# The last additions to x in each mixer: every second one through ScalarE and GpSimd

## The chip, the cores and the metric

The kernel runs on one core of a Trainium2 chip. A core has TensorE (PE, with its weight loads PEld), VectorE (DVE), ScalarE (ACT), GpSimd (POOL) and SyncE (SP), which issues most DMAs. Each engine takes its instructions in the order in which they were written out; semaphores hold one engine back for another. The metric is the device time of one execution in microseconds. Three runs of the kernel before gave 2718.03, 2725.59 and 2727.16 us; the median is 2725.59 us.

## The reference

Two layers work on x, 256 tokens of 2048 features. Layer 0 mixes tokens by sparse attention, layer 1 by an RWKV-7 recurrence, and each mixer is followed by an MLP. What matters here is how a mixer ends and the MLP begins:

```python
    y = mixer(hmix)                       # ends in  o @ w_o
    x = x + g1 * y
    hff = rms_norm(x) * (1 + sc2) + sh2
    x = x + g2 * (jnp.square(jax.nn.relu(hff @ mlp_w1[i])) @ mlp_w2[i])
```

All is float32. The factors g1, sc2 and sh2 come from the conditioning vector through a large matrix (adaLN).

## The kernel before

x lies in SBUF as 16 tiles (x0 to x15, 128 features x 256 tokens). Every float32 product is made of three matmuls: an operand is split into a rounded upper half (hi) and the rest (lo), and the product is hi·hi + hi·lo + lo·hi (`acc3`, L184 to L186). A weight tile is loaded in pieces of 128x512; ScalarE casts each to its hi half (L92), and VectorE or GpSimd subtracts to get its lo half (L94).

The end of a mixer is `out_group` (L451): a block of columns of o times w_o gives 128x256 in PSUM, and L457 on VectorE multiplies it by g1 and adds it to x[f]. The sum over o is cut into blocks, so each x[f] is added to several times, 160 additions in all. The last pass over f = 0 to 15 is the one after which the MLP may use x: in layer 0 the pass over one last tile of o (L732 to L735), in layer 1 the pass over the last two (L841 to L846). In layer 0 the products use five PSUM buffers (`kinds` is `TAIL`), in layer 1 two (`kinds` is "d").

The MLP (`mlp`, L362) needs of each x[f]: h, that is x times a factor in its two halves (hi by L376 on ScalarE, lo by L377 on VectorE), two more columns of h that hold the shift (L372 and L373, GpSimd); and the sum of squares over all f (`tally`: square by L311 on ScalarE, addition by L313 on GpSimd). Each of its first products (`up`, 48 matmuls over the 16 tiles of h) can start before the sum of squares is known, because the norm is applied after it; the root (L289) and its spreading to all partitions (L304 on TensorE) come later. Beside this the adaLN factors of later layers are worked out on VectorE: the sigmoid of c (L208, with a table load, on ScalarE), c times it (L209, 128x2048), then one reduction of 128x2048 after another (L256).

The order on each engine is not the order of the text. A scheduler writes it out from a model of the whole program's course, with priorities where `high_priority` is written. So an edit at one place can move instructions on every engine. Tiles are taken from rings of a fixed number of buffers; a ring's next user waits for its last reader.

Of the kernel before, what the change touches and what calls it, by code (L numbers as in the profile page):

```python
# [11 lines left out]
AF = mybir.ActivationFunctionType  # L12
OP = mybir.AluOpType
# [7 lines left out]
NF = D // P  # L21
# [80 lines left out]
class Trunk:  # L102
# [345 lines left out]
                down(b, g)  # L448
        turn(3)

    def out_group(s, name, layer, block, g, movs, first=0):  # L451

        w = s.wload(s.io[name][block * 4 + g, :, first * 512:(first + len(movs)) * 512])
        for o in range(4):
            f = g * 4 + o
            p = s.dense(w, movs, [k * 512 + o * P for k in range(len(movs))])
            s.nc.vector.scalar_tensor_tensor(s.x[f], p, s.m(layer, 2, f), s.x[f], op0=OP.mult, op1=OP.add)  # L457


    def angles(s, freq, which):  # L460
# [39 lines left out]
    def dsa(s):  # L500
# [65 lines left out]
        p = s.dense(w, h, [k * P for k in range(16)])  # L566
# [153 lines left out]
        last = None  # L720
        for b in range(4):
            om = []
# [7 lines left out]
            last = om  # L730
        s.kinds = TAIL
        for n, o in ((0, om[:3]), (3, om[3:])):  # L732
            for g in range(4):
                s.out_group("a_w_o", 0, 3, g, o, n)
                s.ada(ADA_OUT)  # L735


# [83 lines left out]
    def rwkv_scan(s):  # L821
        todo, om, pre = [], [], []
        for f in range(AHEAD):
            pre.append(s.prepare(f))
            if not f:
                s.pairs()
            if f < AHEAD_INV:
                s.inverse(f, pre[f])
        for f in range(NF):
            cur = pre.pop(0)  # L830
            with s.tc.high_priority(URGENT):
                s.chain(f, cur)
            if f + AHEAD_INV < NF:
                with s.tc.high_priority(URGENT):
                    s.inverse(f + AHEAD_INV, pre[AHEAD_INV - 1])
            if f + AHEAD < NF:
                pre.append(s.prepare(f + AHEAD))
            om.append(s.finish(f, cur))
            if todo and f >= LATE:
                todo.pop(0)()  # L840
            if f in CUTS:  # L841
                todo += [lambda b=f // 4, o=om, g=g, n=f % 4 + 1 - len(om): s.out_group("b_w_o", 1, b, g, o, n)
                         for g in range(4)]
                om = []
        for t in todo:
            t()  # L846
# [453 lines left out]
```

## Time and profile before

| What | Value |
|---|---|
| median of 3 runs | 2725.59 us |
| profiled execution, its own time | 2725.82 us |
| its span, first to last instruction | 2724.0 us |
| mean granted clock | 0.971 |
| PE / PEld busy | 2589.9 us (95%) / 2278.4 us (84%) |
| DVE / ACT / POOL busy | 1832.2 (67%) / 1355.9 (50%) / 1343.7 us (49%) |

The profiled execution is one more execution beside the three runs, 0.2 us above their median. A busy share is an average over the whole span: VectorE's 67% hides stretches where it has no free time. TensorE's matmuls overlap, so the start-to-start distance of two matmuls, not the length of one, says how fast it runs. The time at which a stage ends is read from the timeline, and why an engine stood still from the view of waits.

### The profile page before, as it was taken

How to read it: one execution, taken by the hardware profiler on the slowest of the kernel's cores; microseconds unless marked ns; L12 is line 12 of the kernel's file. 1: busy time of each engine (PE TensorE's matmuls, PEld its weight loads, DVE VectorE, ACT ScalarE, POOL GpSimd, SP SyncE). 2: the span in 40 equal slices, each digit the busy share in tenths (PEclk: the TensorE clock that was granted, in tenths of full speed). 3: DMA queues.
4: the chain of work that ended last, by engine and by line, in shares of the span. 5: the costliest groups of instructions: out<-in, count | busy, mean ns of one | idle time of the engine just before them, and what ended most of it. 6: DMA issues, size and time to landing. Idle time of an engine off the chain costs nothing. (4 is left out here: it accounts for less than half of the span.)

```text
span 2724.0 us, 58482 instructions
## 1 busy us (share of the span) xinstructions
PE 2589.9 (95%) x21996; PEld 2278.4 (84%) x21996; DVE 1832.2 (67%) x2964; ACT 1355.9 (50%) x2963; POOL 1343.7 (49%) x1121
## 2 busy tenths in 40 slices
PE   6899998999999999989899899999799999999997
PEld 4566688988989989879889788888689898898986
DVE  2254468999999999769877565666797354343443
ACT  3434345555555545556655343444455565564553
POOL 1333237576576675755566222233655544444454
PEclk8999999999999999989999898999899999999999
DMA  9998535989999999736476422332585655555553
GB/s 370 410 358 339 202 123 202 325 311 371 319 338 356 318 357 330 261 111 191 140 248 216 161 84 83 99 115 95 193 313 182 215 184 189 189 184 192 186 185 103
DMA packets 263452, 623.30 MB, mean 229 GB/s; under 512 B 29312, under 2 KB 43008, under 8 KB 238336
## 3 DMA queue, kind: packets, MB, share of 16 engines
q1 hardware_dynamic: 256256, 606.98, 64.2%
q10 hardware_dynamic: 6912, 12.59, 1.3%
q8 instruction: 172, 2.82, 0.4%
q14 instruction: 112, 0.92, 0.1%
HBM read 602.67 MB, written 16.78 MB: 227 GB/s over the span
## 5 line engine op out<-in xcount | busy, mean ns | idle before, releaser
L94 POOL TENSOR_TENSOR wlo<-raw,whi 128x512 fp32r<-128x512 f32 x364 | 563.7, 1557 | 538.3 <-ACT whi L92 433.4
L92 ACT CAST whi<-raw 128x512 fp32r<-128x512 f32 x856 | 517.6, 618 | 396.7 <-PE ps_d L185 117.1
L94 DVE TENSOR_TENSOR wlo<-raw,whi 128x512 fp32r<-128x512 f32 x492 | 460.1, 947 | 217.3 <-ACT whi L92 213.6
L94 POOL TENSOR_TENSOR wlo<-more,whi 128x512 fp32r<-128x512 f32 x181 | 274.7, 1520 | 292.3 <-ACT whi L92 236.7
L92 ACT CAST whi<-more 128x512 fp32r<-128x512 f32 x366 | 223.0, 618 | 187.5 <-PE ps_m L418 44.1
L256 DVE CUSTOM_DVE_ANT_0 araw<-araw,cb 128x2048 f32<-128x2048 f32 x112 | 298.1, 2662 | 2.8 <-DMA araw<-ada_w_in 2.6
L94 DVE TENSOR_TENSOR wlo<-more,whi 128x512 fp32r<-128x512 f32 (+1 forms) x185 | 183.6, 995 | 120.4 <-ACT whi L92 117.8
L184 PE MATMUL ps_d<-A,whi 128*128 128x256 f32 x656 | 194.1, 299 | 9.5 <-ACT B L911 5.4
L185 PE MATMUL ps_d<-A,whi 128*128 128x256 f32 x656 | 189.2, 289 | 4.9 <-DVE A L198 4.8
L186 PE MATMUL ps_d<-A,wlo 128*128 128x256 f32 x656 | 188.2, 287 | 0.6 <-DVE wlo L94 0.5
L401 DVE TENSOR_TENSOR A<-B,A 128x256 fp32r<-128x256 f32 x96 | 104.1, 1085 | 99.4 <-ACT A L400 99.1
L185 PE MATMUL ps_d<-h,whi 128*128 128x258 f32 x560 | 160.3, 286 | 8.5 <-DVE h L377 8.5
L184 PE MATMUL ps_d<-h,whi 128*128 128x258 f32 x560 | 159.7, 285 | 0.0
L186 PE MATMUL ps_d<-h,wlo 128*128 128x258 f32 x560 | 158.3, 283 | 0.0
L184 PE MATMUL ps_m<-h,whi 128*128 128x258 f32 x532 | 151.2, 284 | 0.0
L185 PE MATMUL ps_m<-h,whi 128*128 128x258 f32 x532 | 150.8, 284 | 0.0
L184 PEld LDWEIGHTS ps_d<-A,whi 128*128 128x128 f32 x656 | 126.6, 194 | 28.9 <-issue 7.0
L397 ACT ACTIVATE B<-B,sm 128x256 f32<-128x256 f32 x128 | 65.1, 508 | 172.1 <-DVE B L396 172.0
L186 PE MATMUL ps_m<-h,wlo 128*128 128x258 f32 x532 | 149.9, 282 | 0.0
L185 PEld LDWEIGHTS ps_d<-A,whi 128*128 128x128 f32 x656 | 127.1, 194 | 9.1 <-DVE A L198 7.4
L186 PEld LDWEIGHTS ps_d<-A,wlo 128*128 128x128 f32 x656 | 127.1, 194 | 1.9 <-DVE wlo L94 1.0
L94 POOL TENSOR_TENSOR xlo<-more,xhi 128x512 fp32r<-128x512 f32 x51 | 102.0, 2000 | 45.5 <-ACT xhi L92 43.8
(541 smaller groups left out, 8176.4 us busy)
## 6 DMA issues: line engine op xcount, KB each, us to landing
araw<-ada_w_in SPq DMA_DIRECT2D x192, 1024.0 KB, 7.2
raw<-mlp_w_in SPq DMA_DIRECT2D x614, 256.0 KB, 4.2
more<-mlp_w_in SPq DMA_DIRECT2D x410, 256.0 KB, 4.3
raw<-b_w_r_in SPq DMA_DIRECT2D x64, 256.0 KB, 3.2
raw<-b_w_k_in SPq DMA_DIRECT2D x64, 256.0 KB, 3.5
raw<-b_w_v_in SPq DMA_DIRECT2D x64, 256.0 KB, 3.6
raw<-b_w_o_in SPq DMA_DIRECT2D x64, 256.0 KB, 3.3
hd<-A ACTq DMA_DIRECT2D x48, 256.0 KB, 4.0
```

The lines of the kernel that those rows point to most:

```text
L92: t.nc.scalar.copy(hi[:, :n], r)
L94: e.tensor_tensor(lo[:, :n], r, hi[:, :n].bitcast(F32), op=OP.subtract)
L184: mm(out, wh, m[:, :w], start=i == 0, stop=False)
L185: mm(out, wh, m[:, w:], start=False, stop=False)
L186: mm(out, wl, m[:, :w], start=False, stop=i == n - 1)
L256: nc.vector.tensor_tensor_reduce(out=w, in0=w, in1=s.cb, scale=1.0, scalar=0.0, op0=OP.mult, op1=OP.add, accum_out=acc[:, k:k + 1])
L397: nc.scalar.activation(r, u, AF.Relu, bias=c)
L401: nc.vector.tensor_tensor(t[:, S:], q, t[:, :S].bitcast(F32), op=OP.subtract)
```

## The change

In the last pass of each mixer the additions for odd f are made by two instructions: ScalarE scales the product from PSUM into a new tile of the ring B, and GpSimd adds that tile to x[f]. The even ones stay on VectorE. These are 16 of the 160 additions, 8 in each layer.

```diff
-    def out_group(s, name, layer, block, g, movs, first=0):
+    def out_group(s, name, layer, block, g, movs, first=0, last=False):
...
-            s.nc.vector.scalar_tensor_tensor(s.x[f], p, s.m(layer, 2, f), s.x[f], op0=OP.mult, op1=OP.add)
+            if last and f % 2:
+                q = s.B()
+                s.nc.scalar.activation(q, p, AF.Copy, scale=s.m(layer, 2, f))
+                s.nc.gpsimd.tensor_tensor(s.x[f], s.x[f], q, op=OP.add)
+            else:
+                s.nc.vector.scalar_tensor_tensor(s.x[f], p, s.m(layer, 2, f), s.x[f], op0=OP.mult, op1=OP.add)
...
-                s.out_group("a_w_o", 0, 3, g, o, n)
+                s.out_group("a_w_o", 0, 3, g, o, n, last=n == 3)
```

In layer 1 the same argument is passed for the block that ends at f = 15. The scheduler writes a new order. Line numbers of the changed kernel are 5 or 6 higher from here on: the addition on VectorE is L462, the two new instructions are L459 and L460. In the names below, x_66 to x_81 are x0 to x15; araw, cb and acc belong to the adaLN reductions; wlo and xlo are lo halves of weights.

VectorE where layer 1's mixer passes to its MLP, before:

```order
L457 SCALAR_TENSOR_TENSOR x_69<-ps_d,mod_85,x_69 128x256
L209 TENSOR_TENSOR cb<-cb,araw 128x2048
L457 SCALAR_TENSOR_TENSOR x_70<-ps_d,mod_85,x_70 128x256
L377 SCALAR_TENSOR_TENSOR h<-x_68,mod_85,h 128x256
L94 TENSOR_TENSOR wlo<-more,whi 128x512
L457 SCALAR_TENSOR_TENSOR x_71<-ps_d,mod_85,x_71 128x256
L377 SCALAR_TENSOR_TENSOR h<-x_69,mod_85,h 128x256
L377 SCALAR_TENSOR_TENSOR h<-x_70,mod_85,h 128x256
L457 SCALAR_TENSOR_TENSOR x_72<-ps_d,mod_85,x_72 128x256
L256 ISA araw,acc<-araw,cb 128x2048
```

and in the changed kernel, from the last two additions on:

```order
L462 SCALAR_TENSOR_TENSOR x_78<-ps_d,mod_85,x_78 128x256
L462 SCALAR_TENSOR_TENSOR x_80<-ps_d,mod_85,x_80 128x256
L377 SCALAR_TENSOR_TENSOR h<-x_66,mod_85,h 128x256
...
L377 SCALAR_TENSOR_TENSOR h<-x_81,mod_85,h 128x256
L209 TENSOR_TENSOR cb<-cb,araw 128x2048
L256 ISA araw,acc<-araw,cb 128x2048
L256 ISA acc 128x1
L94 TENSOR_TENSOR wlo<-more,whi 128x512
L94 TENSOR_TENSOR xlo<-raw,xhi 128x512
```

The 8 additions now stand in one block, then all 16 lo halves of h, then L209 and the first reduction, and only then the lo halves of the MLP's weights; before, all of these stood mixed between the additions. Layer 0 has the same shape.

ScalarE at the same place, before:

```order
L376 ACTIVATE h<-x_67,mod_85 128x256
L311 ACTIVATE B<-x_67 128x256
L208 ACT_TABLE_LOAD
L208 ACTIVATE araw<-cb 128x2048
L376 ACTIVATE h<-x_68,mod_85 128x256
L311 ACTIVATE B<-x_68 128x256
L92 CAST whi<-more 128x512
L92 CAST whi<-raw 128x512
L376 ACTIVATE h<-x_69,mod_85 128x256
```

and in the changed kernel, where the stretch begins and where it ends:

```order
L459 ACTIVATE B<-ps_d,mod_85 128x256
L311 ACTIVATE ssq<-x_66 128x256
L459 ACTIVATE B<-ps_d,mod_85 128x256 x7
L376 ACTIVATE h<-x_66,mod_85 128x256
...
L208 ACT_TABLE_LOAD
L208 ACTIVATE araw<-cb 128x2048
L311 ACTIVATE B<-x_74 128x256
...
L311 ACTIVATE lsq<-x_81 128x256
L92 CAST whi<-more 128x512
L92 CAST xhi<-raw 128x512 x2
```

All 16 L376 and 7 L311 stand between the scalings and the table load, 8 more L311 between L208 and the first cast of a weight (L92); before, the casts stood among them.

GpSimd where layer 0's mixer passes to its MLP, before:

```order
L94 TENSOR_TENSOR wlo<-raw,whi 128x512 x4
L372 CAST h<-mod_84 128x2 x4
L373 TENSOR_TENSOR h<-mod_84,h 128x2
L372 CAST h<-mod_84 128x2
L373 TENSOR_TENSOR h<-mod_84,h 128x2
```

and in the changed kernel:

```order
L460 TENSOR_TENSOR x_71<-x_71,B 128x256
L94 TENSOR_TENSOR wlo<-raw,whi 128x512
L460 TENSOR_TENSOR x_73<-x_73,B 128x256
L460 TENSOR_TENSOR x_75<-x_75,B 128x256
L460 TENSOR_TENSOR x_77<-x_77,B 128x256
L460 TENSOR_TENSOR x_79<-x_79,B 128x256
L460 TENSOR_TENSOR x_81<-x_81,B 128x256
L372 CAST h<-mod_84 128x2 x4
L373 TENSOR_TENSOR h<-mod_84,h 128x2
```

The eight L460 of a mixer stand ahead of all of L372 and L373, and these ahead of all but one of the 14 L313. Before, nothing of the products stood on GpSimd: L372 followed lo halves of weights in layer 0 and the last work of the recurrence in layer 1. On TensorE the spreading of the root (L304) stands behind 151 matmuls of `up` in layer 0 before and behind 119 now, in layer 1 behind 119 before and 81 now. In the recurrence of layer 1 the order is also another from its start on, with the same instructions.

## Rows read from the trace of the kernel before

**Rows 1.** Busy time by stage: PE, PEld, DVE, ACT, POOL, granted clock, DMA share, GB/s.

```profile
448.75:483.10 34.35, 24.37 (x167) 23.05 (x166) 34.35 (x37) 18.24 (x44) 29.63 (x22) 0.90 0.61 212
480.00:870.00 390.00, 387.45 (x2523) 354.62 (x2522) 375.11 (x338) 208.39 (x433) 258.99 (x137) 1.00 0.94 337
1945.00:1998.65 53.65, 37.77 (x223) 34.69 (x224) 50.82 (x63) 27.65 (x57) 41.02 (x52) 0.77 0.76 267
```

**Rows 2.** Waits of PE, 441 to 484 us: total us, times, longest.

```profile
PE ps_d L185 <- DVE h L377: 7.0, 2, 3.7
PE ps_d L184 <- DVE x L457: 0.8, 2, 0.5
```

**Rows 3.** Groups by line, PE, 1945 to 1998.65: busy us, mean ns, idle before.

```profile
L184 PE MATMUL ps_d<-o,whi 128*128 128x256 f32 x30 | 11.8, 401 | 13.1 <-DVE x L457 10.1 <-ACT o L197 2.8
```

**Rows 4.** Timeline of PE, layer 0: last product, first matmul behind L304.

```profile
448.62 0.28 PE L186 MATMUL ps_m<-o,wlo 128*128 128x256 f32 x1
...
482.85 0.36 PE L184 MATMUL ps_m<-h,whi 128*128 128x258 f32 x1
```

**Rows 5.** Timeline of PE, layer 1: products, then first matmul behind L304.

```profile
1945.09 0.79 PE L184 MATMUL ps_d<-o,whi 128*128 128x256 f32 x2 [2.82 <-ACT o L197]
...
1949.26 0.37 PE L185 MATMUL ps_d<-o,whi 128*128 128x256 f32 x1
1949.47 0.28 PE L186 MATMUL ps_d<-o,wlo 128*128 128x256 f32 x1
1949.59 0.28 PE L184 MATMUL ps_d<-o,whi 128*128 128x256 f32 x1
...
1981.76 0.41 PE L186 MATMUL ps_d<-o,wlo 128*128 128x256 f32 x1
...
1998.41 0.37 PE L184 MATMUL ps_m<-h,whi 128*128 128x258 f32 x1
```

**Rows 6.** ACT: lines (ns min/median/max), and two pieces of its timeline (us).

```profile
L892 ACT ACTIVATE B<-ps_m,wa x32: 456/465/477, 1356.1 to 1492.3; 128x256 f32<-128x256 f32 x32
453.66 1.69 ACT L376 ACTIVATE h<-x,mod 128x256 fp32r<-128x256 f32 x4
455.26 1.32 ACT L311 ACTIVATE B<-x 128x256 f32<-128x256 f32 x4
L208 ACT ACT_TABLE_LOAD  x2: 1283/1283/1283, 444.2 to 1948.5; - x2
L208 ACT ACTIVATE araw<-cb x2: 1914/1916/1917, 445.5 to 1949.8; 128x2048 f32<-128x2048 f32 x2
```

**Rows 7.** DVE: lines (ns min/median/max), L256 and L94 of layer 1's handover.

```profile
L457 DVE SCALAR_TENSOR_TENSOR x<-ps_d,mod,x x138: 434/481/489, 298.0 to 1983.2; 128x256 f32<-128x256 f32 x138
L377 DVE SCALAR_TENSOR_TENSOR h<-x,mod,h x32: 467/946/1515, 443.8 to 1989.1; 128x256 fp32r<-128x256 f32 x32
L209 DVE TENSOR_TENSOR cb<-cb,araw x2: 2275/2422/2570, 448.9 to 1951.7; 128x2048 f32<-128x2048 f32 x2
L256 DVE CUSTOM_DVE_ANT_0 araw<-araw,cb x9: 2275/2279/3354, 1958.9 to 1998.6; 128x2048 f32<-128x2048 f32 x9
L94 DVE TENSOR_TENSOR xlo<-raw,xhi 128x512 fp32r<-128x512 f32 x3 | 2.0, 683 | 0.1
```

**Rows 8.** POOL: timeline, line, whole-run group, then groups of layer 0's and layer 1's handover.

```profile
1949.92 1.54 POOL L373 TENSOR_TENSOR h<-mod,h 128x2 fp32r<-128x2 f32 x10
L1132 POOL TENSOR_TENSOR fin<-fin,B x16: 724/730/1181, 1594.0 to 1943.9; 128x256 f32<-128x256 f32 x16
L94 POOL TENSOR_TENSOR wlo<-raw,whi 128x512 fp32r<-128x512 f32 x364 | 563.7, 1557 | 538.3 <-ACT whi L92 433.4
L313 POOL TENSOR_TENSOR ssq<-ssq,B 128x256 f32<-128x256 f32 x14 | 13.6, 974 | 3.3 <-DVE x L457 2.5
L313 POOL TENSOR_TENSOR ssq<-ssq,B 128x256 f32<-128x256 f32 x14 | 19.9, 1424 | 8.4 <-ACT B L311 8.0
L94 POOL TENSOR_TENSOR wlo<-raw,whi 128x512 fp32r<-128x512 f32 x4 | 8.0, 1996 | 0.0
```

More of the change, by code (lines that the diff above doesn't have):

```diff
@@ L841, in rwkv_scan @@
             if f in CUTS:
-                todo += [lambda b=f // 4, o=om, g=g, n=f % 4 + 1 - len(om): s.out_group("b_w_o", 1, b, g, o, n)
+                todo += [lambda b=f // 4, o=om, g=g, n=f % 4 + 1 - len(om), l=f == NF - 1:
+                         s.out_group("b_w_o", 1, b, g, o, n, l)
                          for g in range(4)]
```

## Prediction

> **What bounds the kernel now.** I read the busy times by stage first. In the MLP of layer 0 TensorE is busy 387 of 390 us [rows 1]; in such a stretch nothing that another engine saves counts. The two places of the change are exceptions: from the end of layer 0's products to the spreading of the root TensorE is busy 24.4 of 34.35 us, and from the start of layer 1's last products to the same point 37.8 of 53.65 us, with VectorE at 34.35 and 50.8 us, full or nearly so [rows 1]. Then I read the waits there. In layer 0 TensorE waits mainly for L377, the lo half of h (7.0 us), and 0.8 us for the additions themselves [rows 2]. In layer 1 it waits 10.1 us for the additions [rows 3], because only two PSUM buffers hold products and VectorE has reductions of 2.3 to 3.4 us [rows 7] between two additions; the products, begun at 1945.09, end at about 1982 [rows 5]. So the change touches real waits, up to 11 us of them for the additions. Whether TensorE gets the time back is decided by what comes next in the new order, so I follow each engine's queue up to one mark: the first matmul behind L304, at 482.85 us in layer 0 with 151 matmuls of `up` done, and at 1998.41 in layer 1 with 119 done [rows 4, 5].
>
> **What is removed and added.** VectorE loses 16 additions of 0.48 us [rows 7], 7.7 us in all. ScalarE gains 16 scalings; the trace has none of this form, the nearest are activations from PSUM of the same size at 0.46 us, which I take; a step of L311 at 0.33 is the bound below, VectorE's own 0.48 the one above [rows 6, 7], and between them lie 0.15 us per product, less than a PSUM buffer's slack of 0.2 worked out below. GpSimd gains 16 additions of 128x256: 0.73 us undisturbed, 1.42 where VectorE works on SBUF beside it [rows 8]. By themselves these lie beside TensorE; what counts is the queues behind them.
>
> **Layer 1.** Products: 90 matmuls (30 on each of three lines [rows 3]). 18 had started by 1949.47, 0.21 us apart at half clock, when the distance fell to 0.12 [rows 5]. With ScalarE and VectorE emptying one buffer each, 0.48 us of emptying fits beside the next product of six matmuls (0.72), so the other 72 follow at 0.12: 8.6 us, end at 1958.2 instead of 1982. That is 24 us earlier. Call this point T. From T on, ScalarE: one scaling 0.46, 16 L376 at 0.42 and 7 L311 at 0.33 (each a quarter of its row), table load 1.28, L208 1.92: T+12.7; 8 more L311: T+15.3, and only now the first cast of a weight of the MLP [rows 6]. VectorE has finished h by then; L209 waits for L208 and ends at T+15.1, the first reduction at T+17.6 (2.28, or 2.5 with its disturbed ones), the first lo half of a weight at T+18.3 [rows 7]. TensorE has nothing but two matmuls until T+15 and stands until T+18.3: of the 24 us, 18 are gone. Then 77 matmuls come before L304; some 20 of them at half clock, as the 18 were after the pause ahead of 1945.09: 20 x 0.21 + 57 x 0.12 = 11 us, T+29.4 at the earliest. GpSimd may be later: last addition T+1.2, 28 small L372 and L373 at 0.154 to T+5.5, then 14 L313 and 6 lo halves of weights mixed, and the root, which I count as one more addition. Undisturbed, the twelfth L313 ends 0.73 after its square at T+14.3, and 6 x 1.56 + 3 x 0.73 more give T+27; at the durations of this handover before, 5.5 + 12 x 1.42 + 6 x 2.0 + 3 x 1.42 = T+39 [rows 8]. Those durations were measured beside nine reductions and L209 in 53.65 us; in the new order four such stand in this stretch of about 34, 0.12 per us instead of 0.19. I take the middle, T+34: the mark falls at 1958.2 + 34 + 0.5 = 1992.7, but with 81 matmuls done instead of 119. The missing 38 cost 38 x 0.12 = 4.6: 1997.3 against 1998.4, a gain of 1.1 us. The bounds T+29.4 and T+39 give -5.7 and +3.9. SP's queue moves too: three loads for reductions now stand together ahead of the weights' next ones, and the third gets its buffer when the first reduction ends, T+17.6; the pieces behind it belong to the second and third `up` behind the mark, wanted from about T+36 on, so I cost this at nothing; without that cover it would be rival 2's sign.
>
> **Layer 0.** Here five PSUM buffers hold products, and little is won ahead: the 0.8 us of rows 2, so T = 448.74 - 0.8 = 447.9. ScalarE and VectorE have the same queue, T+15.3 and T+18.3. One difference helps: three pieces of the second `up` are ready, so TensorE has 36 matmuls before it stands; they cannot start before GpSimd, which has eight additions and a lo half in its way (8 x 0.73 + 1.56 = 7.4 us from about T-5 on, to about T+3), has written the first shift columns, and they fit into the time before T+15. Behind T+18.3 stand 79 matmuls before L304: 20 x 0.21 + 59 x 0.12 = 11.3, T+29.6. GpSimd: T+3, small ones to T+7.3, 12 L313 at this handover's 0.97 to T+18.9, 5 lo halves at 1.56 to 2.0 and 3 x 0.97 more: T+29.6 to T+32; at layer 1's 1.42, T+38.6 [rows 8]. I take T+32.5: the mark at 447.9 + 32.5 + 0.4 = 480.8 with 119 matmuls instead of 151 at 482.85; the missing 32 cost 3.8: 484.6, a loss of 1.8 us. Bounds: -1.1 and +7.9.
>
> **One rule weighed.** L377 takes 0.47 or about 0.95 us, up to 1.5, while L457, which has only one input in SBUF, never takes more than 0.49; GpSimd's additions spread from 0.73 to 1.42 on the mean [rows 7, 8]. The Trainium skill, page "SBUF — State Buffer", section "Who interferes with whom", says that a VectorE instruction with two SBUF inputs contends with a GpSimd instruction that reads SBUF, one blocking the other wholly, and one with a single SBUF input does not. By that rule the change moves eight additions per layer from a form that disturbs nobody into one that blocks L377; the durations agree with it. It is rival 2 below.
>
> **The sum.** -1.1 + 1.8 = +0.7 us on the profiled execution's 2725.8 (span 2724.0 and 1.8 around it; 0.2 above the median): 2726.5, say 2727. What VectorE saves in busy time is hidden by TensorE's full stretches. The reordered recurrence has the same matmuls; I count 0, with 3 us either way as an estimate, a quarter of the products' wait of rows 3. Added bounds: -6.8 - 3 and +11.8 + 3.
>
> **Rivals.** (1) GpSimd runs undisturbed and ScalarE's queue is hidden by more weights cast early: both handovers at their lower bound, -6.8, and one more pause (T+15 to T+18.3 in layer 1) gone: -10, 2716. For it: 24 us of earlier products in layer 1 are a large reserve. Against it: the casts stand behind 15.3 us of ScalarE's queue by the written order. (2) The shared work of GpSimd and VectorE decides: every L313 and lo half at 1.42 and 2.0 in both layers, L304 at T+39, +11.8: 2737.5. It ends slower; its place is GpSimd's queue between the last L460 and L289, and it decides from about T+34 on, when TensorE has done the matmuls ahead of L304. For it: L313 took 1.42 in layer 1; against it: fewer reductions stand there now. (3) The reordered recurrence or the full VectorE of layer 0's MLP (375 of 390 us [rows 1]) shifts more than the handovers do: 5 us either way, 2722 to 2732, still no change that can be told.
>
> **How the numbers follow.** About 0.3% (8 us) is what a measurement of this kernel can tell from no change. My forecast, near zero, 0.48; rival 3 with no visible change 0.14; rival 1 0.19; rival 2 0.19. Within 0.3% falls 0.62; faster 0.19; slower 0.19. The range reaches to the times of the two side rivals, 2716 to 2738, so that about half of what each holds lies outside.
>
> **What would show it.** Right: in layer 1 the last product near 1958, no wait of TensorE for L462, but one of 15 us or more for a cast or a lo half of a weight (L92, L94); L208 12 to 13 us behind the last scaling; L304 between T+29 and T+39 in both layers, the wait ahead of it on GpSimd's L313 or L289. Wrong: TensorE at work with `up` by T+8 in layer 1 (gain of 10 us and more), products that still wait for buffers, or times past the handovers that shift by more than 5 us.

## The result and the profile after

The changed kernel takes 2742.54 us (median of 6 runs, 2740.64 to 2749.68), the kernel before in the same comparison 2726.98 (6 runs, 2718.03 to 2730.59): a ratio of 1.0064, 95% interval 1.0045 to 1.0083. It is slower by some 16 us, where 2727 and no change were forecast, and above the range (2738). The profiled execution of after took 2749.68 us with a span of 2747.9; it is the longest of the six, so differences to before are read by stretch and not from its whole span.

What the change was to do, it did. First the busy time of after in the two short stretches of [rows 1] (same columns, and from the same events), then the groups of the scalings and of GpSimd's additions (ns minimum, median, maximum, first and last start).

```profile
448.10:491.90 43.80, 23.87 (x132) 22.79 (x132) 26.75 (x33) 22.30 (x50) 40.17 (x59) 0.73 0.60 210
1960.70:2016.90 56.20, 33.84 (x182) 31.99 (x183) 33.23 (x42) 27.23 (x59) 45.25 (x63) 0.66 0.44 150
```

```profile
L459 ACT ACTIVATE B<-ps_d,mod x11: 462/475/477, 443.3 to 1974.4; 128x256 f32<-128x256 f32 x11
L460 POOL TENSOR_TENSOR x<-x,B x16: 717/737/1184, 445.2 to 1974.9; 128x256 f32<-128x256 f32 x16
```

VectorE, full before in the first stretch (34.35 of 34.35 us), is now busy 26.75 of 43.80; the busiest helper engine is GpSimd, 40.17 of 43.80 and 45.25 of 56.20. In both stretches the mean granted clock is lower than in [rows 1], 0.73 and 0.66 instead of 0.90 and 0.77.

The next rows are PE's timeline: in layer 0 the last product, L304 and the first matmul behind it ([rows 4] before), in layer 1 the first and the last product, L304 and the first matmul behind it ([rows 5]); and the group of the layer-1 products on L184 (busy us, mean ns, idle before; [rows 3]).

```profile
447.81 0.28 PE L186 MATMUL ps_m<-o,wlo 128*128 128x256 f32 x1
...
491.53 0.60 PE L304 MATMUL ps_m<-cst,sm 128*128 128x128 f32 x4
491.89 0.37 PE L184 MATMUL ps_m<-h,whi 128*128 128x258 f32 x1
...
1960.70 0.58 PE L184 MATMUL ps_d<-o,whi 128*128 128x256 f32 x1 [2.82 <-ACT o L197]
...
1974.06 0.28 PE L186 MATMUL ps_d<-o,wlo 128*128 128x256 f32 x1
...
2016.57 0.61 PE L304 MATMUL ps_m<-cst,sm 128*128 128x128 f32 x4
2016.93 0.36 PE L184 MATMUL ps_b<-h,whi 128*128 128x258 f32 x1
```

```profile
L184 PE MATMUL ps_d<-o,whi 128*128 128x256 f32 x30 | 10.0, 339 | 3.0 <-ACT o L197 2.8
```

The products of layer 1 take 13.6 us instead of 37, and the 10.1 us that they waited for additions in [rows 3] are gone. The loss lies behind them. To size it I read one more mark, the first product with the MLP's second matrix (L416): how long after the end of the last product it starts in layer 0, and how long after the end of the last transpose of the recurrence in layer 1. PE's timeline at these points, of before (with its first L327 of layer 0, for later: L327 is the matmul that sums the tally over the partitions) and of after:

```profile
466.92 0.28 PE L327 MATMUL ps_m<-cst,ssq 128*128 128x1 f32 x2
...
568.88 0.40 PE L416 MATMUL ps_d<-whi,A 128*128 128x512 f32 x1
...
1941.58 0.69 PE L1128 MATMUL ps_m<-cst,fin 128*128 128x128 f32 x2 [3.98 <-DVE fin L1125]
...
2088.42 0.40 PE L416 MATMUL ps_d<-xhi,A 128*128 128x512 f32 x1
```

```profile
583.32 0.40 PE L416 MATMUL ps_d<-whi,A 128*128 128x512 f32 x1
...
1957.38 0.50 PE L1134 MATMUL ps_m<-cst,fin 128*128 128x128 f32 x2 [3.31 <-DVE fin L1131]
...
2111.45 0.40 PE L416 MATMUL ps_d<-xhi,A 128*128 128x512 f32 x1
```

Layer 0: 568.88 - 448.90 = 119.98 us before, 583.32 - 448.09 = 135.24 after (differences of unrounded times), 15.3 lost. Layer 1: 2088.42 - 1942.27 = 146.15 before, 2111.45 - 1957.88 = 153.57 after, 7.4 lost. Call these two the handover of layer 0 and of layer 1.

What TensorE waited for in them, in layer 0 (440 to 500 us; [rows 2] before) and then in layer 1 (1957 to 2020):

```profile
PE ps_m L327 <- POOL ssq L313: 7.0, 1, 7.0
PE ps_d L184 <- ACT xhi L92: 5.4, 1, 5.4
PE ps_a L184 <- POOL h L372: 4.7, 1, 4.7
PE ps_d L186 <- DVE xlo L94: 1.9, 1, 1.9
```

```profile
PE ps_d L184 <- ACT whi L92: 15.3, 1, 15.3
PE ps_d L186 <- POOL xlo L94: 4.0, 1, 4.0
```

The wait of 7.0 us for L377 in [rows 2] has become one of 7.0 us for the tally (L313), one for ScalarE's first cast and one for the shift columns (L372), which stand behind GpSimd's additions. In layer 1 the wait of 15.3 us for the first cast is the one that was forecast; behind it stands one of 4.0 us for a lo half of a weight (xlo) that GpSimd makes behind a block of tally additions, and none for the tally itself. GpSimd's queue in layer 0 and then in layer 1, each with the first L327; and GpSimd's two groups of L313 (layer 0, layer 1; [rows 8] before), with the eleven of layer 1's block by themselves (1984.65 to 2000.8; ns minimum, median, maximum):

```profile
461.18 16.31 POOL L313 TENSOR_TENSOR ssq<-ssq,B 128x256 f32<-128x256 f32 x11
477.45 3.31 POOL L94 TENSOR_TENSOR wlo<-more,whi 128x512 fp32r<-128x512 f32 x1
480.72 1.16 POOL L313 TENSOR_TENSOR ssq<-ssq,B 128x256 f32<-128x256 f32 x1
481.85 1.26 POOL L94 TENSOR_TENSOR wlo<-raw,whi 128x512 fp32r<-128x512 f32 x1
483.07 0.72 POOL L313 TENSOR_TENSOR ssq<-ssq,B 128x256 f32<-128x256 f32 x1
...
483.84 0.58 PE L327 MATMUL ps_m<-cst,ssq 128*128 128x1 f32 x2 [6.97 <-POOL ssq L313]
```

```profile
1984.70 16.21 POOL L313 TENSOR_TENSOR ssq<-ssq,B 128x256 f32<-128x256 f32 x11
2000.88 1.70 POOL L94 TENSOR_TENSOR xlo<-raw,xhi 128x512 fp32r<-128x512 f32 x1
2002.55 2.77 POOL L313 TENSOR_TENSOR ssq<-ssq,B 128x256 f32<-128x256 f32 x1
2005.28 2.50 POOL L94 TENSOR_TENSOR wlo<-raw,whi 128x512 fp32r<-128x512 f32 x2
2007.74 0.73 POOL L313 TENSOR_TENSOR ssq<-ssq,B 128x256 f32<-128x256 f32 x1
...
2008.91 0.42 PE L327 MATMUL ps_m<-cst,ssq 128*128 128x1 f32 x2
```

```profile
L313 POOL TENSOR_TENSOR ssq<-ssq,B 128x256 f32<-128x256 f32 x14 | 18.1, 1296 | 0.8
L313 POOL TENSOR_TENSOR ssq<-ssq,B 128x256 f32<-128x256 f32 x14 | 19.6, 1403 | 0.8
L313 POOL TENSOR_TENSOR ssq<-ssq,B x11: 723/1057/2667, 1984.7 to 1999.9; 128x256 f32<-128x256 f32 x11
```

In both layers eleven tally additions stand in one block, 1.48 us each on the mean; the last addition of all ends 35.7 us (layer 0) and 34.1 us (layer 1) after the last product, and L327, which sums the tally, starts within half a microsecond of that. In layer 0 TensorE waited 7.0 us for it. In layer 1 it did not wait: its own queue, held up by the first cast and by GpSimd's lo halves, came to L327 0.44 us after the tally's end. L304 starts 7.7 us after L327 in both: behind the eight L327s stand 33 and 31 matmuls of `up` in TensorE's queue.

### The profile page after: what moved, and what is told of

The parts are those of the page before. It is cut to its first block, busy times and chain, and to the rows that moved or that the text cites. A ratio compares the mean times of both kernels' runs of the same rounds, so it can differ in the third digit from the quotient of the medians.

```text
span 2747.9 us, 58487 instructions
## 1 busy us (share of the span) xinstructions
PE 2596.8 (95%) x21996; PEld 2283.3 (83%) x21996; DVE 1817.6 (66%) x2948; ACT 1360.2 (50%) x2979; POOL 1362.3 (50%) x1137
## 3 DMA queue, kind: packets, MB, share of 16 engines
q8 instruction: 172, 2.82, 0.4%
## 5 line engine op out<-in xcount | busy, mean ns | idle before, releaser
L94 POOL TENSOR_TENSOR wlo<-raw,whi 128x512 fp32r<-128x512 f32 x364 | 559.7, 1547 | 563.9 <-ACT whi L92 467.0
L92 ACT CAST whi<-raw 128x512 fp32r<-128x512 f32 x856 | 516.4, 618 | 393.4 <-PE ps_d L185 101.9
L94 DVE TENSOR_TENSOR wlo<-raw,whi 128x512 fp32r<-128x512 f32 x492 | 470.8, 967 | 223.4 <-ACT whi L92 218.7
L94 POOL TENSOR_TENSOR wlo<-more,whi 128x512 fp32r<-128x512 f32 x181 | 278.4, 1540 | 295.3 <-ACT whi L92 225.1
L92 ACT CAST whi<-more 128x512 fp32r<-128x512 f32 x366 | 223.0, 618 | 199.9 <-PE ps_m L418 46.4
L256 DVE CUSTOM_DVE_ANT_0 araw<-araw,cb 128x2048 f32<-128x2048 f32 x112 | 286.8, 2561 | 7.2 <-DMA araw<-ada_w_in 7.1
L94 DVE TENSOR_TENSOR wlo<-more,whi 128x512 fp32r<-128x512 f32 (+1 forms) x185 | 183.3, 993 | 126.5 <-ACT whi L92 125.4
L184 PE MATMUL ps_d<-A,whi 128*128 128x256 f32 x656 | 194.2, 298 | 7.9 <-ACT B L917 4.2
L184 PE MATMUL ps_d<-h,whi 128*128 128x258 f32 x560 | 160.8, 287 | 15.3 <-ACT whi L92 15.3
L184 PE MATMUL ps_m<-h,whi 128*128 128x258 f32 x532 | 151.1, 284 | 0.0
L184 PEld LDWEIGHTS ps_d<-A,whi 128*128 128x128 f32 x656 | 126.3, 193 | 27.4 <-issue 7.0
L94 POOL TENSOR_TENSOR xlo<-more,xhi 128x512 fp32r<-128x512 f32 x51 | 100.8, 1977 | 46.8 <-ACT xhi L92 45.1
```

Of the source, the lines that this page charges most:

```text
L92: t.nc.scalar.copy(hi[:, :n], r)
L94: e.tensor_tensor(lo[:, :n], r, hi[:, :n].bitcast(F32), op=OP.subtract)
L184: mm(out, wh, m[:, :w], start=i == 0, stop=False)
L256: nc.vector.tensor_tensor_reduce(out=w, in0=w, in1=s.cb, scale=1.0, scalar=0.0, op0=OP.mult, op1=OP.add, accum_out=acc[:, k:k + 1])
```

## The experiments

Each of e1 to e12 was timed beside the kernel before, four kernels to a chip. The table has the ratio to before, then by stretch of the profiled run (us): handover of layer 0; from the first to the last L416 of layer 0 (the MLP); from there to the last transpose (layer 1's mixer, mainly the recurrence); handover of layer 1.

| kernel | ratio (95%) | hand. 0 | MLP 0 | mixer 1 | hand. 1 |
|---|---|---|---|---|---|
| before | 1 | 119.98 | 621.2 | 752.2 | 146.15 |
| after | 1.0064 (1.0045 to 1.0083) | 135.24 | 622.2 | 752.4 | 153.57 |
| e1 | 1.0056 (1.0034 to 1.0078) | 135.34 | 621.7 | 748.6 | 143.10 |
| e2 | 1.0041 (1.0017 to 1.0064) | 120.15 | 620.6 | 765.7 | 152.74 |
| e3 | 1.0093 (1.0069 to 1.0117) | 130.70 | 623.8 | 757.4 | 151.31 |
| e4 | 1.0126 (1.0099 to 1.0154) | 136.07 | 632.0 | 752.0 | 153.31 |
| e5 | 1.0054 (1.0034 to 1.0074) | 135.46 | 621.7 | 749.4 | 154.19 |
| e6 | 1.0019 (1.0001 to 1.0037) | 127.54 | 629.1 | 743.2 | 146.48 |
| e7 | 0.9947 (0.9927 to 0.9968) | 115.64 | 621.8 | 754.9 | 128.64 |
| e8 | 1.0093 (1.0064 to 1.0123) | 131.25 | 621.8 | 764.1 | 154.29 |
| e9 | 1.0062 (1.0037 to 1.0086) | 134.89 | 621.8 | 749.0 | 152.66 |
| e10 | 1.0042 (1.0023 to 1.0061) | 121.16 | 626.6 | 757.0 | 141.56 |
| e11 | 1.0064 (1.0042 to 1.0086) | 127.76 | 621.3 | 765.9 | 151.56 |
| e12 | 0.9954 (0.9936 to 0.9973) | 115.04 | 622.0 | 751.6 | 130.59 |

Where the code of a handover is the same, it repeats within 0.6 us in layer 0 (after, e1, e5, e9 and before, e2) and within 1.5 in layer 1 (after, e2, e5), but e1's unchanged layer 1 differs from before by 3. Gains of 2 us in layer 1 are therefore not clear of the scatter. The mixer of layer 1 scatters by 23 us; so a whole time says less about a cause than the handovers do, and I judge by these.

**e1, e2: one layer each.** `last=n == 3` left out of layer 1's call, then of layer 0's:

```diff
-  s.out_group("b_w_o", 1, b, g, o, n, l)              (e1)
+  s.out_group("b_w_o", 1, b, g, o, n)
-  s.out_group("a_w_o", 0, 3, g, o, n, last=n == 3)    (e2)
+  s.out_group("a_w_o", 0, 3, g, o, n)
```

> The change in layer 0 alone; layer 1's last products are added by VectorE as before. Theory Q (queues): because the products are emptied sooner, ScalarE, VectorE and GpSimd do all of h, the squares, the table load and the sigmoid ahead of the first weights of the MLP, TensorE stands and restarts at its lower clock; in the trace after this cost layer 0 14.9 us up to the first product of the second MLP matrix, so 2736 to 2742. Rival G (GpSimd's additions, sharing with VectorE, are what costs): the eight additions per layer cost about the same in either layer, half of 15.6 us: 2735. Rival R (the time is lost in the reordered recurrence or in the MLP, not in the handover): 2727 to 2730 with the MLP of layer 0 starting on time.

> The change in layer 1 alone. Theory Q: in the trace after this handover is 7.9 us later against the last transpose of the recurrence, of which an early restart of the products has paid 14; 2728 to 2735, with a wait of TensorE of 15 us for a cast of a weight. Rival G: 2735. Rival R: the recurrence moves too, 2735 to 2740.

Each part alone makes its own handover slow (135.34 and 152.74) and leaves the other. The loss is in the handovers and not in layer 0's MLP, and layer 0's share is about twice layer 1's.

**e3: VectorE adds in GpSimd's place.**

```diff
-  s.nc.gpsimd.tensor_tensor(s.x[f], s.x[f], q, op=OP.add)
+  s.nc.vector.tensor_tensor(s.x[f], s.x[f], q, op=OP.add)
```

> As the changed kernel, but the second half of each odd addition (x plus the scaled product) on VectorE instead of GpSimd; the order behind the products in layer 1 is the same as in the changed kernel. Theory Q: 2738 to 2745, since the queues behind the products are the same, with TensorE's wait of about 15 us for the first cast in layer 1 still there; layer 0 can lose up to 3 us less, because the shift columns don't wait behind GpSimd's additions. Rival G: back to 2725 to 2730, with the squares' additions on GpSimd near 0.75 us instead of 1.48.

PE's waits in layer 0 of e3:

```profile
PE ps_m L327 <- POOL ssq L313: 6.1, 1, 6.1
PE ps_d L184 <- ACT xhi L92: 4.8, 1, 4.8
PE ps_a L185 <- POOL h L373: 2.8, 2, 2.6
```

4.5 us come back in layer 0: the additions on GpSimd are a part of the loss there, not all of it. The 2.3 in layer 1 are not clear of the scatter. The tally stays late without them (it ends 33.3 and 31.8 us after the last product), and L313 stays at 1.30 and 1.38 us, so rival G's 0.75 is refuted. The whole time did not improve (1.0093); e3's mixer of layer 1 was 5 us longer, which is not enough to explain that.

**e4: TensorE kept busy.**

```diff
+  pw = s.bank("j")
+  for t in ts:
+      for k in range(7):
+          nc.tensor.matmul(pw[:, :S], t[:, :P], t[:, :S], start=True, stop=True)
```

> As the changed kernel, with 112 extra matmuls per layer (seven on each tile of h, into a buffer that nobody reads) in the time in which TensorE stands. If the lower clock after the standstill is part of the loss (some 70 matmuls 0.21 us apart instead of 0.12 in layer 1, about as many in layer 0), the restart is at full clock and up to 6 us per layer come back, less what GpSimd's tally then makes it wait: 2733 to 2738. If the lateness of GpSimd's tally alone decides, 2741 to 2744. If the extra matmuls delay the first useful ones, 2745 to 2755.

Neither handover gets shorter, and the MLP of layer 0 takes 10 us longer, with 5.6 us of waits for VectorE's lo halves of weights in it. The extra matmuls were done before TensorE waited again, so this run did not settle the clock; e9 repeats it with more.

**e5: the change again.**

> The changed kernel itself once more, so that the other kernels of this call stand beside it on one chip. From the two halves measured apart (15.2 and 11.2 us slower) 2735 to 2750; from its own first measurement 15.6 us above the kernel before. Its two handovers, from the last product to the first product of the MLP's second matrix in layer 0 and from the last transpose of the recurrence to the same point in layer 1, should again be near 135 and 153 us (119.98 and 146.15 before), whatever the whole time does.

The handovers repeat within 0.6 us, the whole with 1.0054. From the first L327 to L304 it takes 8.1 us in layer 0 and 6.3 in layer 1 here, so the 7.7 of after is itself good to about 1.5 us.

**e6, e7: a late sigmoid, with the change and without it.** The sigmoid gets a bias of zero times a number that is known only when `up` 0 is done, so that the scheduler can't put it, L209 and the first reductions in the handover:

```diff
+  z = s.small(1)
+  nc.vector.tensor_scalar(z, t, 0.0, None, op0=OP.mult)
-  nc.scalar.activation(sg, s.cb, AF.Sigmoid)
+  nc.scalar.activation(sg, s.cb, AF.Sigmoid, bias=z)
...
+  if b == f == 0:
+      s.spread_c(c)
```

> The changed kernel with the sigmoid of c (and with it L209, the first reductions and their three loads in the SP queue) held back by a data dependence until the first column of `up` 0 has been read; the additions to x are those of the changed kernel. Theory Q: ScalarE's queue ahead of the first cast is 3.2 us shorter, VectorE's ahead of the first lo half 8 us shorter, GpSimd's tally runs without reductions beside it, the weights' loads aren't held in the SP queue: 8 to 14 us back in layer 0 and as many in layer 1, 2715 to 2728. Rival G (GpSimd's additions ahead of h are the loss): at most 3 us per layer back, 2736 to 2743. Rival D (the reductions held back make VectorE late in layer 0's MLP, in which it is busy 375 of 390 us): the handovers gain as in Q and the MLP of layer 0 loses it again, 2728 to 2735.

> The kernel before (all additions on VectorE) with the same late sigmoid. Theory Q: in layer 1 no reduction of 2.3 to 3.4 us stands between two additions any more, so the products end early without ScalarE's and GpSimd's help, and weights are cast between the h as before: 8 to 15 us faster than before, 2708 to 2716. Rival G makes no difference here. Rival D: no gain, 2720 to 2728.

GpSimd's tally in layer 1 of e6 (its L317 is L313), then TensorE's waits in layer 1 of e7 (1942 to 1990; L464 is the addition, L381 the lo half of h):

```profile
L317 POOL TENSOR_TENSOR ssq<-ssq,B 128x256 f32<-128x256 f32 x14 | 12.6, 902 | 0.6
```

```profile
PE ps_d L184 <- DVE x L464: 2.3, 6, 0.6
PE ps_b L185 <- DVE h L381: 0.6, 1, 0.6
```

With the change (e6) 7.7 and 7.1 us come back in the two handovers, the tally addition falls from 1.40 to 0.90 us, and layer 0's MLP takes 6.9 us longer than in after, 5.8 us of it in waits for VectorE's lo halves, as rival D had it. The late sigmoid alone doesn't do that: e7 has it too, and its MLP takes 621.8. Without the change (e7) the kernel is faster than both, 0.9947: the same waits that the change aimed at fall from 10.1 to 2.3 us once no reduction stands between two additions, and ScalarE still casts weights between the h, as the code before has it. With the sigmoid late in both, the change costs 11.9 and 17.8 us, though neither handover has a reduction any more: in layer 1 of e6 TensorE still waits 12.5 us for the first cast, in e7 not at all. So the sigmoid and the reductions are not what makes the changed order slow; they lie on top of it.

**e8: weights first.**

```diff
+  first = [s.wload(s.io["mlp_w1"][layer, f]) for f in range(1)]
   h = []
```

> The changed kernel with the weights of the first `up` asked for ahead of h in the code, so that in layer 1 two pieces are cast ahead of h and two between the squares; in layer 0 the order changes little. Theory Q: TensorE starts on `up` some 6 to 10 us earlier in layer 1 and gains 4 to 8 us there, unless GpSimd's tally then makes it wait; layer 0 the same: 2730 to 2738. If GpSimd's tally alone decides, the same as the changed kernel, 2738 to 2745.

Layer 0 gets 4.0 us back, layer 1 nothing (154.29). In layer 1 the two pieces that were cast ahead of h are not the first that TensorE wants, and its wait for the first cast is still 13.3 us: the experiment did not do what it was made for, and is no verdict on theory Q. It shows something else: its tally in layer 1 ends 44.6 us after the last product, ten later than in after, and the handover is hardly longer: 162 matmuls of `up` stand ahead of its L304 instead of 81. How late the tally is counts only together with how much TensorE has to do ahead of it.

**e9: TensorE kept busy for longer**, in layer 1 alone, eleven matmuls on each tile of h:

> The changed kernel with 176 extra matmuls on the tiles of h in layer 1 alone (into a buffer that nobody reads), so that TensorE works from the first h to about 7 us past the first cast, not only up to it. If the lower clock after the standstill costs what its distances say (about 65 matmuls at 0.21 instead of 0.12), the stretch from the last transpose of the recurrence to the first product of the MLP's second matrix falls from 154 to 147 to 150 us. If GpSimd's and VectorE's lo halves and the tally set the end, it stays at 152 to 156, and if the extra work itself is in the way, 157 or more. Layer 0 as in the changed kernel, 135. The whole: 2737 to 2752.

Stretches of e9 (columns as in [rows 1]; the first begins at the last product), then its last tally addition and L327, and the matmul that waits for GpSimd's lo half, in e9 and in after:

```profile
1968.70:1980.00 11.30, 10.39 (x87) 10.39 (x88) 7.07 (x16) 11.27 (x26) 10.68 (x36) 1.00 0.34 106
1980.00:1992.00 12.00, 12.00 (x104) 12.00 (x103) 11.00 (x8) 8.59 (x19) 11.37 (x9) 1.00 0.53 197
1992.00:1997.00 5.00, 1.84 (x17) 1.64 (x15) 5.00 (x5) 0.62 (x1) 4.92 (x4) 1.00 0.00 0
1997.00:2002.00 5.00, 3.99 (x21) 3.69 (x22) 2.06 (x2) 1.03 (x2) 5.00 (x3) 0.66 0.63 204
```

```profile
2002.07 0.73 POOL L313 TENSOR_TENSOR ssq<-ssq,B 128x256 f32<-128x256 f32 x1
2002.86 0.38 PE L327 MATMUL ps_m<-cst,ssq 128*128 128x1 f32 x2 [0.47 <-POOL ssq L313]
```

```profile
1996.96 0.58 PE L186 MATMUL ps_d<-h,xlo 128*128 128x258 f32 x1 [3.16 <-POOL xlo L94]
```

```profile
2002.64 0.58 PE L186 MATMUL ps_d<-h,xlo 128*128 128x258 f32 x1 [4.00 <-POOL xlo L94]
```

The clock is full for 23 us in which it was low or TensorE stood, and the handover gains 0.9 us against after and 1.5 against e5, no more than the scatter. In both kernels the same matmul waits for GpSimd's xlo and goes on 28.3 us after the last product, and the tally ends 34.1 us after it (2002.80 in e9). So the lower clock after the standstill does not set the end in layer 1; GpSimd's queue, its lo halves and the tally, does. What an earlier first cast would give was not measured: e9 fills the standstill, but its first useful matmul is no earlier.

**e10: late sigmoid and VectorE's additions** (the edits of e6 and e3 together).

> The changed kernel with the late sigmoid and, for the odd additions, ScalarE's scaling and VectorE's sum: GpSimd has nothing of the additions. Theory Q with GpSimd's queue as part of it: in layer 0 the waits of 6.7 us for the shift columns that stood behind GpSimd's additions go, and the stretch from the last product to the second matrix falls from 127.5 to 120 to 124 us; in layer 1, where TensorE's wait is for ScalarE's first cast (12.5 us), it stays at 145 to 148. The whole 2722 to 2730. If GpSimd's additions don't matter, layer 0 stays at 127.

Layer 0 gains 6.4 us on e6, as forecast; layer 1 gains 4.9, which was not. The whole does not follow: 1.0042, where e6 had 1.0019.

**e11: half of the tally on VectorE.**

```diff
-  s.nc.gpsimd.tensor_tensor(s.ssq, s.ssq, q, op=OP.add)
+  if half and f % 2:
+      s.nc.vector.tensor_tensor(s.lsq, s.lsq, q, op=OP.add)
+  else:
+      s.nc.gpsimd.tensor_tensor(s.ssq, s.ssq, q, op=OP.add)
```

> The changed kernel with seven of the fourteen additions of each tally that leads an MLP moved from GpSimd to VectorE. If the lateness of GpSimd's tally is part of the loss, TensorE's wait of 7 us for it in layer 0 goes and 3 to 6 us come back there (129 to 132 instead of 135), and 1 to 4 in layer 1: 2734 to 2741. If VectorE, which has the lo halves and reductions to do, is late in its place: 2742 to 2748.

7.5 us come back in layer 0, half of its loss. The 2.0 in layer 1, where VectorE's half is then late itself (PE's wait for it: 3.8 us), are not clear of the scatter. The whole stays at 1.0064, with a mixer of layer 1 that took 766 us in the profiled run.

**e12: before with late sigmoid, last products of layer 1 in five PSUM buffers.**

```diff
+  k=TAIL if f == NF - 1 else s.kinds:
+  (setattr(s, "kinds", k), s.out_group("b_w_o", 1, b, g, o, n))
```

> The kernel before with the late sigmoid, and with the last output products of layer 1 in five PSUM buffers instead of two (all additions on VectorE). If VectorE's additions behind two buffers still hold the products, they end 13 to 16 us after they start instead of 22, and 2 to 6 us come off: 2708 to 2714. If earlier products only make ScalarE run h and squares ahead of the first casts, as in the change, nothing or a loss: 2714 to 2722.

The products end 16.0 us after they start, 22.4 in e7, and the handover is no shorter (130.59 against 128.64). Earlier products alone are worth nothing here, and they cost little: ScalarE's casts of the MLP's weights begin behind five h (L380 in this kernel), not behind all sixteen as in the changed kernel.

## Why the prediction was wrong

The reading of the waits, the edits and the queues held in the main; layer 0's waits for the first cast (5.4 us) and the shift columns (4.7) were not priced. Products of layer 1: 13.1 us from their start to T forecast (1945.09 to 1958.2), 13.6 measured. First cast at T+15.3: 1988.95 is T+14.6. First lo half of a weight in layer 1 at T+18.3: T+17.5. Matmuls of `up` ahead of L304: 119 and 81, as the order had them. What the missing 32 and 38 matmuls cost behind the mark: 3.8 and 4.6 us forecast, 5.4 and 4.5 measured. Nearly the whole error is the time of the mark after T:

| mark after the last product | forecast | bound | measured |
|---|---|---|---|
| layer 0 (T+32.5 and 0.4) | 32.9 | 39.0 | 43.8 |
| layer 1 (T+34 and 0.5) | 34.5 | 39.5 | 42.6 |

So the step that failed is "I take the middle, T+34" and "I take T+32.5". It has two faults.

The first and larger one is that GpSimd's queue and TensorE's 79 and 77 matmuls were worked out side by side, the later one setting the mark, with the root costed as one more addition behind the tally and half a microsecond from it to the mark. But L327 stands inside TensorE's queue, 33 and 31 matmuls ahead of L304. These can't run while L327 waits for the tally, so the two add up: from L327 to L304 7.69 us in layer 0 (483.84 to 491.53) and 7.66 in layer 1, mostly at the lower of the two clock levels (0.21 us apart; the granted clock of the two stretches was 0.61 and 0.56), after TensorE had stood or waited. The root was mis-sized too: it needs L327 and an instruction on VectorE (L287), and GpSimd's L289 stands behind three more lo halves of weights, so that it is done 4.4 and 5.3 us after the tally. TensorE's queue was still 3.4 and 2.8 us longer than that and set L304. Against the forecast's 1.2 to 1.9 us from the last tally addition to the mark, measured are 8.1 and 8.5: 6.6 to 7.3 us of each of the two errors of 10.9 and 8.1. The instruction order and one row showed this; I read the order only for the count of matmuls. In the trace of before L327 starts at 466.92 in layer 0, 15.6 us ahead of L304 (482.49), and nothing waits for the tally, so that there the place of L327 cost nothing; in layer 1 of before it was 7.0 us ahead of L304 (1990.96 to 1997.94), with the root done just before L304.

The second is the size of GpSimd's work in layer 0. The tally there was costed at that handover's own 0.97 us; it took 1.30 on the mean and 1.48 in its block, so the last addition ends at T+35.7 and not near T+31.5. The argument for a lower rate, fewer reductions per microsecond, counted only the reductions. Beside the block of L313 in layer 1 VectorE ran L209, two reductions and six lo halves of weights, without a pause from 1986.62 on. The single additions of that block show what each does: 0.72 us while VectorE stands still, about 2.65 for the three that meet L209 (2.56 us) or a reduction (2.70 and 2.82), about 1.05 for the rest. In e6, with the sigmoid, L209 and the reductions gone, the longest takes 1.18 in layer 1 and the mean is 0.91 and 0.90. The tally then ends 5.1 and 3.5 us earlier; what else gives the 7 us per layer was not separated. The Trainium skill, page "SBUF — State Buffer", section "Who interferes with whom", which the prediction weighed, names a shared port for which GpSimd contends with VectorE instructions that have two SBUF inputs, and not with those that have one. The trace agrees: L313 takes 2.65 us beside L209 and the reductions, with two, and L460 in layer 1 0.735 us beside additions with one.

Of the rivals, (2) came nearest and was given 0.19. Its place, GpSimd's queue between the last L460 and L289, was right. Its time, 2737.5, came as near as it did in part by luck: it puts the tally's end near T+37 in both layers, later than the 35.7 and 34.1 measured, and has the same short way from there to the mark as the forecast. The sign that the prediction named, L304 between T+29 and T+39, failed in both layers (T+43.4 and T+42.2).

Theory Q, with which the experiments began, is half answered. In layer 1 the standstill until T+15 is real, but GpSimd's lo halves and tally come later still, so that with GpSimd's queue as it is, an earlier first cast can bring L327 at most 0.44 us forward. Why GpSimd's queue is late is known only in parts. It holds h's shift columns, the tally and lo halves behind the additions, and VectorE's reductions fall beside it. e3, e6 and e11 each take one part away, and 4.5 to 7.7 us come back in layer 0, 2.0 to 7.1 in layer 1; e10 takes two, and gets 14.1 and 12.0. The rest, 11.9 and 17.8 us between e7 and e6 with no reductions in either, belongs to the moved additions and the order that comes with them; without GpSimd's additions (e10) 5.5 and 12.9 are left. In layer 1 of e6 and e10 all of h and the squares still stand ahead of the first cast, and that is the likely reason there, though no run has the moved additions with early casts. Earlier products are not the reason for that order: in e12 they are nearly as early, the casts stand among the h, and the handover is within 2 us of e7's. What in the change made the scheduler put h first was not tested. In layer 0 the shift columns behind GpSimd's additions are one more part (4.7 us of waits; e3 gets 4.5 back, e10 6.4 on e6, both with an earlier tally too).

That SP's queue could be costed at nothing was right as far as the waits show. In layer 1 the three loads for reductions did hold SP until 1992.28, and ScalarE waited 4.1 us for the piece whose load stood behind them. The longer wait, 7.3 us for the next piece, had another reason: SP itself waited for a buffer that GpSimd's late xlo still read (waits of SP, 1965 to 2015).

```profile
SPq L167 <- POOL xlo L94: 9.2, 1, 9.2
```

TensorE waited for neither piece by the view of its waits. No run separates the loads.

Open is how the handovers add up to the whole. In the two profiled executions they do: the handovers of after lose 22.7 us, and the spans differ by 23.9. But the medians differ by 15.6 only, and e3, e10 and e11 get 6.8, 26.1 and 9.5 us back in the handovers while their ratios are 1.0093, 1.0042 and 1.0064. The scatter of the mixer between kernels is of the size of these gaps for e11 (13.5 us longer than in after) and not for e3 and e10 (5 us); that it is the reason was not shown.

## What to carry to other kernels

To take work off a full engine pays only if the engine that waits finds something to do next: follow the queue of the waiting engine past the next barrier, and add, not overlap, whatever stands in that queue behind an instruction that has to wait. When instructions move to other engines, the queues behind them are written anew, and the work there can pile up where it was spread before: read the new order of each helper engine up to the point where the waiting engine needs it. Here it paid to move a deferrable piece (the sigmoid and the reductions that hang on it) out of the handover by a dependence, 0.9947 of before, with no addition moved at all.

## What the runs showed of the hardware

The mixer of layer 1 runs the same number of matmuls in all kernels, but took from 743 to 766 us, and longer where the granted clock is lower. e6, before and e2 in that stretch (columns as in [rows 1]):

```profile
1201.90:1945.10 743.20, 695.09 (x9662) 627.36 (x9660) 540.03 (x1289) 363.20 (x910) 310.51 (x357) 0.96 0.45 142
```

```profile
1190.10:1942.30 752.20, 701.91 (x9662) 631.38 (x9660) 540.98 (x1289) 365.14 (x910) 307.72 (x357) 0.94 0.43 140
```

```profile
1188.90:1954.70 765.80, 716.99 (x9662) 644.39 (x9660) 541.20 (x1289) 364.92 (x910) 307.64 (x357) 0.92 0.43 137
```

9662 matmuls each, at 0.96, 0.94 and 0.92 of the full clock. VectorE's and ScalarE's busy times agree within 2 us. That the clock is the cause of the longer times, and not the other way round, was not shown. A change of a few microseconds elsewhere in this kernel is hidden by this in any single execution.
